# Q, K and V of a hybrid decoder layer: one PSUM bank per half product, the next pair's resident products between streamed ones

## The chip, the cores and the metric

One Trainium2 chip, of which the kernel uses one core. The metric is the device time of one execution in microseconds (us), lower is better. A comparison is made between runs of both kernels on the same chip.

A core has five engines, each with a queue of its own that it works off in order: TensorE (PE in the profile; PEld is its weight loads), VectorE (DVE), ScalarE (ACT), GpSimd (POOL) and SyncE (SP), which here issues all DMAs. [...] Operands lie in SBUF.

## The reference

One layer on 1040 tokens (16 meta tokens and 1024 of `x`), width 1024. The part that the change is about:

```python
xn = rms_norm(h, mix_pre_g[l])
proj = xn @ w_in[l]
...
q = proj[..., OFF_Q:OFF_K].reshape(Bsz, L, SB_HEADS, SB_HEAD_DIM)
k = proj[..., OFF_K:OFF_V].reshape(Bsz, L, SB_HEADS, SB_HEAD_DIM)
v = proj[..., OFF_V:IN_COLS].reshape(Bsz, L, SB_HEADS, SB_HEAD_DIM)
y_ssd = ssd_mixer(z, xbc, dt_raw, conv_w, ...)
y_sb = rms_norm(stick_breaking_attention(q, k, v).reshape(Bsz, L, SB_WIDTH), sb_norm_g[l])
mix = jnp.concatenate([y_ssd, y_sb], axis=-1) @ w_out[l]
```

After it come a residual, and a convolutional feed-forward of 2816 columns with its own norms. `ssd_mixer` is a scan over chunks of 128 tokens; the attention takes, for each query, a product of sigmoids over the keys behind it.

## The kernel before, in words

Float32 products are made of three passes: each operand is split into a high part (`fp32r`) and the rest (`lo`), and high x high, high x low and low x high are summed. ScalarE makes the high part, GpSimd or VectorE the rest.

**Stages.** x is normed and turned (lines 227 to 340) into `xall`, which holds both parts of all 1040 tokens; `xq` is a view of it by block of 128 columns of x, half of the tokens, part and token. Then the projections for the scan of head group 0 (line 877), the scan of group 0 with projections of group 1 as filler (878 to 885), the scan of group 1 with Q, K and V as filler (888 to 891), the attention with the rest of Q, K and V as filler (1156 to 1212), the output projection and the feed-forward.

**Q, K and V** are made two 128-column blocks at a time: 12 pairs (`Blocks`, line 400), in the order (k, q), (v, q), (k, v) for every two head pairs. One pair times x is a 2 x 2 block product (two blocks of output, two halves of the inner dimension; two halves of the tokens), done by Strassen's scheme in Winograd's form with 7 products instead of 8. `QKV` (line 45) gives their order, 1, 2, 6, 5, 3, 7, 4, with the names of their operands. Each is done in two halves `c` of 260 tokens: 14 half products, *steps*, a pair; 168 in all. A step is 12 matmuls of 128 x 128 on 128 x 260 (line 497). What is called M5c0 below is product 5, half 0.

Products 1, 2 and 3 read x itself from `xq` (the operands `b11`, `b21`, `b22`): they are *resident*. Products 6, 5, 7 and 4 read sums of x's quarters (`t2`, `t1`, `t3`, `t4`), which were written to DRAM once (`x_sums`, line 360, to `xt13` and `xt42`) and are *streamed* back: each half product needs one unit of 1040 KB, in two halves. They land in a ring of two units (line 388), which lies where the fourth quarter of x was. `load_half` (392) is called twice in every streamed step, behind the matmuls that read the half to be replaced, and so always loads for the streamed step after next.

PSUM has two banks for this (`psum_mm`, line 75, two buffers), one for each `c`. Products 1 and 2 add up in one bank, 5 and 3, and 7 and 4 too: the flag `first` says which of them starts a sum. Between them the bank is read: after 1 ScalarE copies it to C21 (508), and after 2 the same bank holds C11. VectorE adds the others to what is in SBUF (514 to 525). For a K block, high part and rest are made straight from PSUM (`keep_k`, 470): ScalarE copies, and VectorE subtracts; the list `late` puts these behind the next step's matmuls.

**Weights.** A pair's two raw blocks (512 KB each) are loaded into two buffers (`load`, 405, `wraw`), sums are made of them in place on VectorE (`sums`, 425), and four splits make high part and rest (`split_a`, `split_s12`, `split_s34`, `split_a22`; ScalarE line 413, GpSimd line 414) into three rotating buffers. `qkv_flow` (571) says after which of a pair's 14 steps each of these is put into the program: `split_s34` after step 1 and `split_a22` after step 5 of the pair itself; for the next pair `load(0)` after 3, `load(1)` after 8, `split_a` after 9, `sums` after 10, `split_s12` after 12.

**The order of the work.** In the attention TensorE runs in the order in which the program is written (line 1154). For the other engines and for SP the framework's scheduler chooses an order when the kernel is built: of what it takes to be ready, the earliest in the program. So a load whose buffer it takes to be free can come to stand ahead of loads that are written before it. An engine's queue is then worked off in that order, and an instruction that waits holds up all behind it. `behind` (351) keeps the operations of `x_sums` from going ahead of what was written before on the named engines.

**The attention** takes one block of 128 queries of one head pair at a time (`block_weights`, 920): logits on TensorE (940), two sigmoids on ScalarE (941, 942), a scan on VectorE (948), a product on GpSimd (950, 951); the turning (962) and the product with V (977) come up to three blocks later. Two or three steps of Q, K and V go into each (`run(fill, 1)`). When a head pair is done, the last of it is added up on VectorE (1000) and stored (1001). `turn_v` and `turn_edge` (535, 546) turn V for it.

Of the kernel before, what the change touches and what calls it, by code (L numbers as in the profile page):

```python
# [44 lines left out]
QKV = [(1, "a11", "b11", True), (2, "a12", "b21", False), (6, "s2", "t2", True), (5, "s1", "t1", True),  # L45
       (3, "s4", "b22", False), (7, "s3", "t3", True), (4, "a22", "t4", False)]
# [11 lines left out]
def tile_layer(ctx: ExitStack, tc: tile.TileContext, x, meta, rows, parts,  # L58
# [292 lines left out]
    def behind(*engines):  # L351
        st = ExitStack()
        traced = nc.cur_bb.bb.instructions
        for e in engines:
            last = next((i for i in reversed(traced) if i.engine == e), None)
            if last is not None:
                st.enter_context(tc.issue_after(last))
        return st

    def x_sums(k):  # L360
        rs = []

        def add_up():
            rs.extend(rp.tile([P, 2, HT], F32R, tag="rkl", name=f"xr{j}_{k}", bufs=3).bitcast(F32) for j in range(2))
            r1, r2 = rs
            with behind(ET.Pool):
                for r, kk in ((r1, k), (r2, k + 4)):
                    nc.gpsimd.tensor_tensor(r, xq[:, kk, :, 0].bitcast(F32), xq[:, kk, :, 1].bitcast(F32), op=ALU.add)
                nc.gpsimd.tensor_tensor(r1[:, 0], r1[:, 1], r1[:, 0], op=ALU.subtract)
                nc.gpsimd.tensor_tensor(r1[:, 1], r2[:, 1], r1[:, 1], op=ALU.subtract)  # L370

        def split():
            r1, r2 = rs
            with behind(ET.DVE, ET.Activation):
                nc.vector.tensor_tensor(r2[:, 1], r2[:, 1], r1[:, 0], op=ALU.subtract)
                nc.vector.tensor_tensor(r2[:, 0], r2[:, 0], r2[:, 1], op=ALU.subtract)
                for r, dst, nm in ((r1, xt13, "13"), (r2, xt42, "42")):
                    h = rp.tile([P, 2, HT], F32R, tag="rk", name=f"xh{nm}_{k}", bufs=3)
                    lo = r.bitcast(F32R)
                    nc.scalar.activation(h, r, AF.Copy)  # L380
                    nc.vector.tensor_tensor(lo, r, h.bitcast(F32), op=ALU.subtract)
                    for j, s in enumerate((h, lo)):
                        nc.sync.dma_start(out=dst[:, :, :, k, j, :],
                                          in_=s.bitcast(F32).rearrange("p t (c n) -> p t c n", n=HP))

        return add_up, split

    ring = [xq[:, 0:4, 1].rearrange("p k b n -> p k (b n)")[:, :, 2 * HP * s:2 * HP * s + 2 * HP] for s in range(2)]
# [3 lines left out]
    def load_half():  # L392
        u, h = divmod(loaded[0], 2)
        if u < len(units):
            loaded[0] += 1
            (src, j), c = t_of[units[u][0]], units[u][1]
            ks = slice(2 * h, 2 * h + 2)
            nc.sync.dma_start(out=ring[u % 2][:, ks].bitcast(F32), in_=src[:, j, c, ks].rearrange("p k b n -> p k (b n)"))

    class Blocks:  # L400
        def __init__(self, f1, f2, n):
            self.n, self.src, self.w = n, [{"q": w_q, "k": w_k, "v": w_v}[f][p] for f, p in (f1, f2)], {}
            self.f, self.r, self.late = (f1, f2), [None, None], []
# [21 lines left out]
        def sums(self):  # L425
            r1, r2 = self.r
            self.s2 = rp.tile([P, 4, P], F32, tag="s2", name=f"s2_{self.n}", bufs=1)
            add = nc.vector.tensor_tensor
            add(r1[:, 0:4], r1[:, 0:4], r2[:, 0:4], op=ALU.subtract)
# [34 lines left out]
        def part(self, j, th, c):  # L464
            a = HT * th + HP * c
            if self.f[j][0] == "k":
                return [t[:, a:a + HP] for t in self.d[j]]
            return self.d[j][:, a:a + HP]

        def keep_k(self, th, c, a):  # L470
            kh, kl = self.part(0, th, c)
            acts = [lambda: nc.scalar.activation(kh, a, AF.Copy),
                    lambda: nc.vector.tensor_tensor(kl, a, kh.bitcast(F32), op=ALU.subtract)]
            if th == 0:
                acts.pop(0)()
            self.late += acts

        def step(self, s):
            (n, wn, xn, first), c = QKV[s // 2], s % 2
            if s == 0:  # L480
                self.d = [None, self.dest(1)]
            if s == 2:
                self.d[0] = self.dest(0)
            if first:
                self.acc = getattr(self, "acc", {})
                self.acc[c] = psum_mm(f"pj{n}_{self.n}_{c}")
            acc = self.acc[c]
            hi, lo = self.w[wn]
            if xn[0] == "t":
                rv = ring[used[0] % 2].rearrange("p k (b n) -> p k b n", b=2)  # L490
                used[0] += 1
            else:
                kk, th = {"b11": (0, 0), "b21": (4, 0), "b22": (4, 1)}[xn]
                rv = xq[:, kk:kk + 4, th, :, HP * c:HP * c + HP]
            for k in range(4):
                for j, (w, b) in enumerate(((hi, 0), (hi, 1), (lo, 0))):
                    mm(acc[:, :HP], w[:, k, :], rv[:, k, b, :], start=first and k == 0 and j == 0,  # L497
                       stop=k == 3 and j == 2, skip_group_check=not first)
                if xn[0] == "t" and k % 2:
                    load_half()  # L500
            for act in self.late:
                act()
            self.late = []
            add, a = nc.vector.tensor_tensor, acc[:, :HP]
            c11 = self.part(0, 0, c) if n in (2,) else None
# [3 lines left out]
            elif n == 2 and self.f[0][0] == "k":  # L509
                self.keep_k(0, c, a)  # L510
            elif n == 2:
                nc.scalar.activation(c11, a, AF.Copy)
            elif n == 6:
                add(c21, a, c21, op=ALU.add)
            elif n == 5:
                add(c22, a, c21, op=ALU.add)
            elif n == 3 and self.f[0][0] == "k":
                add(a, a, c21, op=ALU.add)
                self.keep_k(1, c, a)
            elif n == 3:  # L520
                add(self.part(0, 1, c), a, c21, op=ALU.add)
            elif n == 7:
                add(c22, a, c22, op=ALU.add)
            elif n == 4:
                add(c21, a, c21, op=ALU.add)
# [19 lines left out]

    def turn_edge(p):
        q, (kh, kl), v, vc = heads[p]
        vt = vts.pop(p)
        edge = rp.tile([P, NT, NM], F32, tag="edge", name=f"edge{p}", bufs=1)
        nc.vector.tensor_copy(edge[:, :NT - 1, :], vt[:, P:NT * P].rearrange("p (t c) -> p t c", c=P)[:, :, :NM])  # L550
        nc.vector.tensor_copy(edge[:, NT - 1, :], vt[:, T:L])
        tp = psum_tp(f"vtc{p}")
        nc.tensor.transpose(tp[:, 0, :], edge.rearrange("p t c -> p (t c)"), ident)
# [6 lines left out]
    def v_turns(p):  # L560
        return [lambda: turn_v(p, 0), lambda: turn_v(p, 1), lambda: turn_edge(p)]
# [9 lines left out]
    def qkv_flow():  # L571
        post = []
        for n, b in enumerate(blocks):
            nxt = blocks[n + 1] if n + 1 < len(blocks) else None
            (f1, p1), (f2, p2) = b.f
            for s in range(14):
                b.step(s)
                if post and s:
                    post.pop(0)()
                if s == 1:  # L580
                    b.split_s34()
                if s == 5:
                    b.split_a22()
                if nxt:
                    ahead = {3: lambda: nxt.load(0), 8: lambda: nxt.load(1), 9: nxt.split_a, 10: nxt.sums,
                             12: nxt.split_s12}.get(s)
                    if ahead:
                        ahead()
                if s == 9 and f1 == "v":
                    post = v_turns(p1)  # L590
                if nxt is None:
                    left[0] = 2 * ((s > 0) + (s > 2) + (s > 8) + (s > 12))
                    left[1] = int(s > 8)
                yield
            if f2 == "v":
                post = v_turns(p2)
        for act in post[:2] + [lambda: None] * 2 + post[2:]:
            act()
            yield
# [13 lines left out]
    with tc.tile_pool(name="ssd", bufs=1, side="right") as sp:  # L613
# [248 lines left out]
        def scan_steps(g):  # L862
# [3 lines left out]
            for c in range(NT + 1):  # L866
# [7 lines left out]
        parts_ = [x_sums(k) for k in range(4)]  # L874
        posts = [[parts_[0][0]], [parts_[0][1], parts_[1][0]], [parts_[1][1], parts_[2][0]],
                 [parts_[2][1], parts_[3][0], parts_[3][1]]]
# [31 lines left out]
    edges, ys_of = {}, {}  # L908
# [84 lines left out]
    def edge_mix(p, th):  # L993
# [7 lines left out]
        nc.sync.dma_start(out=yd1[:, :, p, :].rearrange("t d c -> d t c"), in_=ysc)  # L1001
# [154 lines left out]
    for p in range(8):  # L1156
        for i in range(NT):
# [11 lines left out]
            run(block)  # L1169
            if (p, i) == (7, 1):  # L1170
# [50 lines left out]
    edge_mix(7, edge)  # L1221
    run(meta_steps)
# [837 lines left out]
```

## Time and profile before

| | us |
|---|---|
| median of 3 runs | 1852.49 |
| lowest, highest | 1851.43, 1856.2 |
| the profiled execution | 1856.6 |
| its span, first to last instruction | 1854.8 |
| start of the first and the last matmul of Q, K and V (line 497) | 335.2, 935.4 |
| granted TensorE clock, mean over the span | 0.968 |

The profile is of one execution. Times in it are counted from the span's start. A row of a group names line, engine, operation, output<-input, shape and count, then its busy time and the mean of one, then the time that the engine stood idle just before it, and who ended that. A row of waits has the total, how often, and the longest. The time of the profiled execution is 4.1 us over the median of the runs.

### The profile page before, as it was taken

The numbers are of one execution on the slowest core, as the hardware profiler recorded it, in microseconds if no ns is written. First come the engines' busy times: TensorE is split into PE (matmuls) and PEld (weight loads), VectorE is DVE, ScalarE is ACT, GpSimd is POOL, SyncE is SP. The second block draws the span as 40 slices with busy tenths as digits, with TensorE's granted clock in tenths as the row PEclk, the third lists the DMA queues.
The fourth block names the chain that finished last, engine by engine and source line by source line (L and its number), as shares of the span: only waits on it lengthen the run. The fifth ranks groups of instructions, "written<-read, shape, count | busy, mean of one in ns | idle before, by whom it ended". The sixth has DMA issues, their size and how long they took to land. (4 is left out here: it accounts for less than half of the span.)

```text
span 1854.8 us, 29414 instructions
## 1 busy us (share of the span) xinstructions
PE 1729.7 (93%) x11518; PEld 1508.0 (81%) x11518; DVE 1233.3 (66%) x1360; ACT 856.6 (46%) x1474; POOL 972.9 (52%) x697
## 2 busy tenths in 40 slices
PE   7999899997888889888899999999999999999998
PEld 6998789876777788777767877898888999888786
DVE  5765884776658758768764056766666666657777
ACT  5424463543555656546665234543333333334544
POOL 4365664575657747667546212458677777600001
PEclk9999899998999989999999999999999999999999
DMA  4235443677665556655722354423223333187335
GB/s 153 69 109 177 146 132 103 206 251 244 216 199 185 196 158 200 218 201 192 239 92 83 133 198 148 137 69 117 95 86 92 118 103 104 61 270 251 103 97 187
DMA packets 151354, 284.73 MB, mean 154 GB/s; under 512 B 14032, under 2 KB 47336, under 8 KB 151216
## 3 DMA queue, kind: packets, MB, share of 16 engines
q1 hardware_dynamic: 151216, 282.85, 46.3%
q8 instruction: 91, 1.49, 0.3%
q14 instruction: 47, 0.39, 0.1%
HBM read 224.56 MB, written 58.25 MB: 152 GB/s over the span
## 5 line engine op out<-in xcount | busy, mean ns | idle before, releaser
L950 POOL TENSOR_TENSOR bt<-bt,kp 128x256 f32<-128x256 f32 (+7 forms) x128 | 210.2, 1660 | 139.9 <-DVE kp L948 110.3
L948 DVE TENSOR_TENSOR_SCAN kp<-kp,hold 128x272 f32<-128x272 f32 (+7 forms) x128 | 209.4, 1676 | 64.6 <-ACT kp L941 47.6
L497 PE MATMUL pj<-xall,whis 128*128 128x260 f32 x768 | 169.9, 319 | 53.0 <-DMA xall<-xt 35.1
L497 PEld LDWEIGHTS pj<-xall,whis 128*128 128x128 f32 x768 | 131.3, 209 | 69.3 <-issue 26.0
L1413 POOL TENSOR_TENSOR wlo<-wr,whi 128x1024 fp32r<-128x1024 f32 x43 | 109.2, 2551 | 37.2 <-ACT whi L1412 37.2
L497 PE MATMUL pj<-xall,whia 128*128 128x260 f32 x576 | 116.3, 300 | 10.2 <-DMA xall<-xt 6.2
L1917 POOL TENSOR_TENSOR fms<-fms 128x1 f32<-128x1 f32 x8 | 2.7, 334 | 223.7 <-DMA ar<-fda 187.5
L497 PE MATMUL pj<-xall,wlos 128*128 128x260 f32 x384 | 116.2, 303 | 0.0
L941 ACT ACTIVATE kp<-z 128x288 f32<-128x288 f32 (+6 forms) x112 | 82.5, 737 | 67.5 <-PE z L940 33.0
L497 PEld LDWEIGHTS pj<-xall,whia 128*128 128x128 f32 x576 | 89.8, 192 | 21.0 <-issue 6.0
L1412 ACT ACTIVATE whi<-wr 128x1024 fp32r<-128x1024 f32 x43 | 45.6, 1060 | 112.5 <-PE fX L1470 68.1
L160 PE MATMUL pj_X<-xall,wh_X 128*128 128x320 f32 (+1 forms) x384 | 96.9, 338 | 0.0
L1542 DVE SCALAR_TENSOR_TENSOR ga<-gr,pp,ga 128x1024 f32<-128x1024 f32 x44 | 71.4, 1622 | 34.0 <-ACT ga L1535 33.1
L964 ACT ACTIVATE th<-tw 128x1024 f32<-128x1024 f32 (+2 forms) x96 | 75.8, 815 | 39.2 <-PE tw L962 37.9
L160 PE MATMUL pj_z<-xall,wh_z 128*128 128x306 f32 (+2 forms) x384 | 92.4, 327 | 0.0
L1802 ACT ACTIVATE dh<-ar 128x512 fp32r<-128x512 f32 x77 | 48.5, 630 | 92.5 <-PE dnB L1880 44.7
L1803 DVE TENSOR_TENSOR dl<-ar,dh 128x512 fp32r<-128x512 f32 x77 | 53.2, 691 | 50.4 <-ACT dh L1802 50.3
L1119 PE MATMUL mo<-xall,yh 128*128 128x512 f32 x256 | 85.7, 402 | 0.0
L962 PE MATMUL tw<-ident,bt 128*128 128x128 f32 x576 | 78.7, 280 | 5.4 <-ACT bt L942 3.1
L942 ACT ACTIVATE bt<-z 128x288 f32<-128x288 f32 (+6 forms) x112 | 82.8, 740 | 0.0
L497 PE MATMUL pj<-xall,wloa 128*128 128x260 f32 x288 | 81.7, 284 | 0.0
L497 PEld LDWEIGHTS pj<-xall,wlos 128*128 128x128 f32 x384 | 80.3, 209 | 0.0
(579 smaller groups left out, 5752.6 us busy)
## 6 DMA issues: line engine op xcount, KB each, us to landing
xall<-xt SPq DMA_DIRECT2D x192, 520.0 KB
wr<-in_w_up SPq DMA_DIRECT2D x44, 512.0 KB
fds<-ga SPq DMA_DIRECT2D x44, 256.0 KB
b<-in_w_down SPq DMA_DIRECT2D x44, 256.0 KB
ar<-fds SPq DMA_DIRECT2D x44, 256.0 KB
fda<-ga SPq DMA_DIRECT2D x33, 256.0 KB
ar<-fda SPq DMA_DIRECT2D x33, 256.0 KB
yk<-yd SPq DMA_DIRECT2D x16, 512.0 KB
```

What stands on the lines that cost most here:

```text
L160: mm(acc[:ncol, :n - s], a[:, k, :ncol], x_cols(k, b, c0 + s, n - s), start=(k == 0 and j == 0), stop=(k == KB - 1 and j == 2))
L497: mm(acc[:, :HP], w[:, k, :], rv[:, k, b, :], start=first and k == 0 and j == 0, stop=k == 3 and j == 2, skip_group_check=not first)
L941: nc.scalar.activation(kp[:, :, a:a + w], z[:, :, :w], AF.Sigmoid, scale=-QSCALE)
L942: nc.scalar.activation(bt[:, :, a:a + w], z[:, :, :w], AF.Sigmoid, scale=QSCALE)
L948: nc.vector.tensor_tensor_scan(kp[:, j][:, ::-1], kp[:, j][:, ::-1], hold[:, L - n:L][:, ::-1], 0.0, op0=ALU.mult, op1=ALU.max)
L950: nc.gpsimd.tensor_tensor(bt[:, j, 0:m], bt[:, j, 0:m], kp[:, j, 1:m + 1], op=ALU.mult)
L962: nc.tensor.transpose(tw[:, j, b, :], bt[:, j, c0:c0 + P], ident)
L964: nc.scalar.activation(th[:, :, :nb, :], tw[:, :, :nb, :], AF.Copy)
L1119: mm(acc, u[:, k, :], v[:, cs], start=(k == 0 and j == 0), stop=(k == 7 and j == 2))
L1413: nc.gpsimd.tensor_tensor(l, raw, h.bitcast(F32), op=ALU.subtract)
L1542: nc.vector.scalar_tensor_tensor(v, self.g[jj][:, :, i:i + 256], fconv_w[:, j, i:i + 1], v, op0=ALU.mult, op1=ALU.add)
L1803: sub(lo[:, k], raw, hi[:, k].bitcast(F32), op=ALU.subtract)
```

## The change

- **Banks.** Each half product starts a sum in a bank of its own, and the bank is free when it has been read once. Products 2 and 3 now get their other term by an add on VectorE; product 7 is added to both C22 and C21. For a K block one add on VectorE empties the bank into a float32 tile `ks` (it shares the one buffer `s2` with the weights' sum S2), and for both halves together ScalarE makes the high part and GpSimd the rest.
- **Order.** From the first pair on, products 1 and 2 of the next pair are done within this one: 6, 5, 3, 7, next 1, 4, next 2. The counting of steps starts at product 6.
- **Weights.** `split_a22` after step 1 (M6c1), `load(0)` after 2, `split_a` after 4, `load(1)` after 5, `sums` after 7, `split_s12` after 9, `split_s34` of the next pair after 12.
- **Half units.** The ring is four pieces; a half unit is 128 runs of 4160 bytes where it was 256 of 2080.
- **x's sums.** All operations of `x_sums` run on VectorE, without `behind`; its tiles alternate between two tags; all of one k is put behind one z block.
- **Smaller.** The columns of V that the last turn needs are copied out right after the second turn (`keep_edge`); the store of a head pair's result (1001) is put behind the rest of the block's logits; when the output projection's weights may overwrite x follows the new order.

```diff
-            with behind(ET.Pool):
-                for r, kk in ((r1, k), (r2, k + 4)):
-                    nc.gpsimd.tensor_tensor(r, xq[:, kk, :, 0].bitcast(F32), xq[:, kk, :, 1].bitcast(F32), op=ALU.add)
...
-                    nc.scalar.activation(h, r, AF.Copy)
+        op2 = nc.vector.tensor_tensor
+        for r, kk in ((r1, k), (r2, k + 4)):
+            op2(r, xq[:, kk, :, 0].bitcast(F32), xq[:, kk, :, 1].bitcast(F32), op=ALU.add)
+        op2(r1[:, 0], r1[:, 1], r1[:, 0], op=ALU.subtract)
+        op2(r1[:, 1], r2[:, 1], r1[:, 1], op=ALU.subtract)
+        op2(r2[:, 1], r2[:, 1], r1[:, 0], op=ALU.subtract)
+        op2(r2[:, 0], r2[:, 0], r2[:, 1], op=ALU.subtract)
+        for r, dst, nm in ((r1, xt13, "13"), (r2, xt42, "42")):
...
+            nc.vector.tensor_copy(h, r)
+            op2(lo, r, h.bitcast(F32), op=ALU.subtract)
...
-    ring = [xq[:, 0:4, 1].rearrange("p k b n -> p k (b n)")[:, :, 2 * HP * s:2 * HP * s + 2 * HP] for s in range(2)]
+    ring = [xq[:, a, 1].rearrange("p b n -> p (b n)") for a in range(4)]
...
-            nc.sync.dma_start(out=ring[u % 2][:, ks].bitcast(F32), in_=src[:, j, c, ks].rearrange("p k b n -> p k (b n)"))
+            nc.sync.dma_start(out=ring[2 * (u % 2) + h].bitcast(F32), in_=src[:, j, c, ks].rearrange("p k b n -> p (k b n)"))
...
+        def keep_k(self, th, c, a, term):
+            if c == 0:
+                self.ks = rp.tile([P, HT], F32, tag="s2", name=f"ks{th}_{self.n}", bufs=1)
+            nc.vector.tensor_tensor(self.ks[:, HP * c:HP * c + HP], a, term, op=ALU.add)
+            if c == 1:
+                kh, kl = (t[:, HT * th:HT * th + HT] for t in self.d[0])
+                nc.scalar.activation(kh, self.ks, AF.Copy)
+                nc.gpsimd.tensor_tensor(kl, self.ks, kh.bitcast(F32), op=ALU.subtract)
...
-            if first:
-                self.acc = getattr(self, "acc", {})
-                self.acc[c] = psum_mm(f"pj{n}_{self.n}_{c}")
-            acc = self.acc[c]
+            acc = psum_mm(f"pj{n}_{self.n}_{c}")
...
+            if n in (2, 3):
+                term = c21 if n == 2 else c22
+                if self.f[0][0] == "k":
+                    self.keep_k(n - 2, c, a, term)
+                else:
+                    nc.vector.tensor_tensor(self.part(0, n - 2, c), a, term, op=ALU.add)
+                return
+            for dst, term in {6: ((c21, c21),), 5: ((c22, c21),), 7: ((c22, c22), (c21, c21)), 4: ((c21, c21),)}[n]:
+                nc.vector.tensor_tensor(dst, a, term, op=ALU.add)
...
+            row = [(b, 6), (b, 5), (b, 3), (b, 7)] + ([(nxt, 1), (b, 4), (nxt, 2)] if nxt else [(b, 4)])
+            acts = {1: [b.split_a22]}
...
+                acts.update({4: [nxt.split_a], 7: [nxt.sums], 9: [nxt.split_s12], 12: [nxt.split_s34]})
...
+                acts[2] = [lambda: nxt.load(0)]
+                acts[5] = [lambda: nxt.load(1)]
...
-        nc.sync.dma_start(out=yd1[:, :, p, :].rearrange("t d c -> d t c"), in_=ysc)
+        stores.append(lambda: nc.sync.dma_start(out=yd1[:, :, p, :].rearrange("t d c -> d t c"), in_=ysc))
...
             run(block)
+            while stores:
+                stores.pop()()
```

More of the change, by code (lines that the diff above doesn't have):

```diff
@@ L499, in step @@
                 if xn[0] == "t" and k % 2:
                     load_half()
[L501 to L505, printed above, removed]
+            a = acc[:, :HP]
             c21, c22 = self.part(1, 0, c), self.part(1, 1, c)
```

166 lines of the change are left out of this document (69 added, 97 removed).

## Prediction

> **What bounds the kernel now.** First the head of the page and its row of busy times:
>
> ```profile
> span 1854.8 us, 29414 instructions
> ...
> PE 1729.7 (93%) x11518; PEld 1508.0 (81%) x11518; DVE 1233.3 (66%) x1360; ACT 856.6 (46%) x1474; POOL 972.9 (52%) x697
> ```
>
> TensorE is busy for 93%, so time is to be won where it stands still. The table by stretches, for the 600 us of Q, K and V, has PE, PEld, DVE, ACT, POOL, granted clock, DMA share:
>
> ```profile
> 335.00:935.00 600.00, 517.54 (x4372) 456.70 (x4371) 431.30 (x505) 332.85 (x635) 393.95 (x299) 0.93 0.64 211
> ```
>
> TensorE stands still for 82.5 us, most of its idle time in the kernel, and the clock is 0.93 where the whole run has 0.968. Who ended those waits say the groups of line 497 (`whis` are the weights of products 6, 5, 3, 7; `whia` those of 1, 2, 4) and the waits:
>
> ```profile
> L497 PE MATMUL pj<-xall,whis 128*128 128x260 f32 x768 | 169.9, 319 | 53.0 <-DMA xall<-xt 35.1 <-DVE kl L473 16.0 <-DVE vt L521 1.0
> L497 PE MATMUL pj<-xall,whia 128*128 128x260 f32 x574 | 115.9, 300 | 10.2 <-DMA xall<-xt 6.2 <-DVE q L525 2.2 <-DVE q L523 1.3
> ```
>
> ```profile
> PE pj L497 <- DVE kl L473: 16.0, 10, 2.9
> ...
> PE pj L497 <- DVE q L525: 2.2, 2, 1.9
> ...
> PE pj L497 <- DVE q L523: 1.3, 1, 1.3
> PE pj L497 <- DVE vt L521: 1.0, 2, 0.8
> PE pj L497 <- DVE q L516: 0.8, 1, 0.8
> ...
> PE pj L497 <- DVE vt L525: 0.5, 1, 0.5
> ```
>
> The ring costs 41.3 us (35.1 under `whis`, 6.2 under `whia`, where only product 4 is streamed), the emptying of banks 21.8. Why the ring is late shows one pair, on the queues of SP, POOL and PE:
>
> ```profile
> 578.96 0.35 SPq L407 DMA_DIRECT2D wr<-in_w_k  x1
> 590.19 0.35 SPq L407 DMA_DIRECT2D wr<-in_w_q  x1
> 590.63 8.04 SPq L398 DMA_DIRECT2D xall<-xt  x6
> ```
>
> ```profile
> 588.73 1.43 POOL L414 TENSOR_TENSOR wloa<-wr,whia 128x512 fp32r<-128x512 f32 x1
> ```
>
> ```profile
> 595.35 0.77 PE L497 MATMUL pj<-xall,whis 128*128 128x260 f32 x2 [5.47 <-DMA xall<-xt]
> ```
>
> `load(1)` of the next pair stands ahead of the loads for M5c0, although it is written four steps behind them. Its buffer comes free when GpSimd ends `split_a22` (590.16); until then SP stands, the ring's loads behind it, and M5c0 waits 5.47 us. So it is the queue's order and GpSimd's lateness, not the bandwidth. Over the stage:
>
> ```profile
> SPq L407 <- POOL wlos L414: 61.9, 10, 12.5
> SPq L407 <- POOL wloa L414: 57.6, 7, 16.1
> ...
> SPq L1001 <- DVE ysc L1000: 17.6, 6, 7.1
> ```
>
> **The change part by part.** The profiled execution took 1856.6 us, 1.8 of it outside its span; the runs' median is 4.1 lower. The sum starts from 1856.6.
>
> *Product 4.* Its units are asked for two steps ahead as before, but with the next pair's product 1 between 7 and 4, two resident steps lie there: four steps. The 6.2 us go: **-6.2** (ends 0 and -6.2). What would be late next, the next pair's M6, also has four steps.
>
> *Products 6 and 5* stay four streamed steps in a row, so M5 still gets its unit two steps after it is asked for. `split_a22` may begin when product 2 ends, and M6 follows product 2 in both kernels: what held up the ring at 590 is still there. Against that, more work for GpSimd lies just ahead of that place (`split_s34` and the rest of K), which the scheduler sees too; where it takes the buffer to come free later, it puts `load(1)` behind the ring's loads, as it did in this earlier pair:
>
> ```profile
> 535.52 1.06 SPq L398 DMA_DIRECT2D xall<-xt  x2
> 536.72 0.38 SPq L407 DMA_DIRECT2D wr<-in_w_v  x1
> 539.78 8.41 SPq L398 DMA_DIRECT2D xall<-xt  x6
> ```
>
> Ends: all 35.1 gone, or each of 11 pairs 1.5 us later (the next paragraph's K rest) and so 16 more. I take 27 left, **-8**. Single pieces carry the same bytes in half the runs; the ring waits for its queue, so nothing is counted. The store of line 1001, moved behind the block, stood ahead of ring loads for part of its 17.6 us; that is within the same ends.
>
> *Banks.* The rest of K was held back by a step and kept its bank: 16.0. Now one add frees it. What other adds cost is 5.8 us (2.2, 1.3, 1.0, 0.8, 0.5) for 104 of them; with 144 banks freed by VectorE I scale to 8.0: **-13.8** (ends: -21.8 and 0, when VectorE is late for all). The adds:
>
> ```profile
> L414 POOL TENSOR_TENSOR wlos<-s,whis 128x512 fp32r<-128x512 f32 x11 | 16.4, 1495 | 6.5 <-ACT whis L413 6.5
> L473 DVE TENSOR_TENSOR kl<-pj,kh 128x260 fp32r<-128x260 f32 x32 | 13.4, 420 | 8.3 <-ACT kh L472 8.3
> L429 DVE TENSOR_TENSOR wr<-wr,wr 128x512 f32<-128x512 f32 x11 | 10.0, 909 | 13.1 <-POOL wloa L414 13.1
> L948 DVE TENSOR_TENSOR_SCAN kp<-kp,hold 128x144 f32<-128x144 f32 (+7 forms) x110 | 181.7, 1692 | 39.6 <-ACT kp L941 35.5 <-issue 2.0 <-POOL bt L950 1.8
> L950 POOL TENSOR_TENSOR bt<-bt,kp 128x128 f32<-128x128 f32 (+7 forms) x110 | 177.7, 1634 | 105.9 <-DVE kp L948 81.2 <-ACT ysc L980 7.0 <-ACT bt L942 5.5
> L917 DVE TENSOR_TENSOR ql<-q,qh 128x128 fp32r<-128x128 f32 x57 | 63.8, 1120 | 1.5 <-ACT qh L916 1.4
> ```
>
> A K pair has 14 adds on VectorE before and after (four subtractions go, two adds for product 2 and two for 7 come; product 3 keeps its two), the four others 10 and 14: 16 x 0.42 = 6.7 us more in 431, beside TensorE. GpSimd gets 16 rests of K, 520 wide: 16 x 1.5 = 24 us more in 394. On the path comes only what waits for it: `sums`, whose tile shares its buffer with `ks`. It stands in VectorE's queue ahead of scans, and GpSimd waits for those. The like wait in the row of line 429 is 13.1; I take **+4** (ends 0 and 13).
>
> *Clock.* Behind a long wait TensorE runs at half clock; the stretch behind the wait at 590:
>
> ```profile
> 594.00:600.00 6.00, 4.65 (x26) 4.20 (x28) 0.43 (x1) 0.64 (x2) 0.00 (x0) 0.50 0.98 353
> ```
>
> 0.07 of 600 us is 42 us of clock withheld for 82.5 idle; part of it falls on the idle time itself, so I take 0.3 us per us of wait: on 28 us removed **-8.5** (ends 0 and -14, all of it). [...]
>
> *What the others take back.* With 36.5 us less of waits and slow clock, VectorE's 431 and GpSimd's 394 have to fit into less time. I let them take back half: **+18** (ends 0 and all).
>
> *x's sums.*
>
> ```profile
> L368 POOL TENSOR_TENSOR xr<-xall x8: 2400/2650/3434, 98.7 to 188.3; 128x1040 f32<-128x1040 f32 x8
> L380 ACT ACTIVATE xh<-xr x8: 1057/1071/1075, 148.3 to 197.7; 128x1040 fp32r<-128x1040 f32 x8
> L381 DVE TENSOR_TENSOR xr<-xr,xh x8: 1226/1236/3379, 149.4 to 199.4; 128x1040 fp32r<-128x1040 f32 x8
> ...
> L369 POOL TENSOR_TENSOR xr<-xr x4: 1652/1966/2292, 104.9 to 179.5; 128x520 f32<-128x520 f32 x4
> L370 POOL TENSOR_TENSOR xr<-xr,xr x4: 1302/1742/2293, 107.3 to 192.1; 128x520 f32<-128x520 f32 x4
> L375 DVE TENSOR_TENSOR xr<-xr,xr x4: 700/2568/2917, 125.1 to 193.5; 128x520 f32<-128x520 f32 x4
> L376 DVE TENSOR_TENSOR xr<-xr x4: 701/1988/2392, 127.4 to 195.2; 128x520 f32<-128x520 f32 x4
> ```
>
> ```profile
> PE sg L784 <- ACT sgh L775: 7.6, 3, 4.3
> ```
>
> ```profile
> 100.00:155.00 55.00, 52.21 (x327) 51.73 (x326) 28.82 (x20) 13.13 (x21) 27.39 (x14) 0.97 0.38 124
> 155.00:215.00 60.00, 47.96 (x260) 42.31 (x260) 47.46 (x37) 29.69 (x61) 44.83 (x24) 0.83 0.55 175
> ```
>
> They last to 199, into the scan's first chunks, where TensorE idles 12 of 60 us at clock 0.83 and waits 7.6 for ScalarE, whose queue holds the copies. On VectorE one k is 2 + 2 + 2 operations of 1040 at 1.24 and 4 of 520 at 0.70, 10.2 us, 41 in all (the plain copy's price is not in the trace: at most that of the subtraction). Without `behind` they may fill the 26 us that VectorE idles before 155. GpSimd is rid of 8 x 2.65 + 4 x 1.97 + 4 x 1.74 = 36, ScalarE of 8.6. **-6** (ends -20, the 12 idle us and the clock, and +6, if the last k stands ahead of the first chunk).
>
> Sum: -6.2 - 8 - 13.8 + 4 - 8.5 + 18 - 6 = -20.5, so 1836.1 against the profiled execution and **1832** against the median.
>
> **The rivals.**
>
> *The ring's loads go first.* `load(1)` comes behind them in all pairs. For: the pair at 536. Against: most later pairs look like 590. Another 27 us and their clock, half taken back: 17 less, 1815.
>
> *Nothing to see.* Waits move to other engines. For: the scans already wait 35.5 us for ScalarE and GpSimd 81.2 for the scans. What is left is x's sums and some of product 4: 1848.
>
> *GpSimd late at the pair's edge: slower.* Between M4 and M6 lie two steps now (product 2 alone) where there were four, and at them `split_s34` (whose end frees the buffer of `load(0)`), the rest of K and `split_a22`. The row below gives 2.3 for the first (two shapes in one mean); with 1.5 for the rest of K the last ends 3.8 us later, both loads stand ahead of the ring on SP, and M5 waits 11 x 3.8 = 42 more. With the 20 of product 4 and the banks gone that is +22, +6.6 of clock, half of it caught up by the other engines: +14, +4 and -6: 1864. It decides once GpSimd ends `split_a22` 2 us later than now in most pairs.
>
> ```profile
> L414 POOL TENSOR_TENSOR wlos<-wr,whis 128x1024 fp32r<-128x1024 f32 (+1 forms) x23 | 53.0, 2305 | 18.1 <-ACT whis L413 18.1
> ```
>
> *Two readers of SBUF.* Scans, rests of Q and GpSimd's work sum to 640 us in 600 (181.7 + 63.8 + 393.95), and line 381 takes 1.24 or 3.38 by what runs beside it. If that rate is a ceiling, 24 us more make the stage 600 x 664/640 = 622, and TensorE's waits only move: +22 - 6, 1868. [...]
>
> **How the numbers follow.** Forecast 0.44 (its own range 1815 to 1846), loads first 0.11, nothing 0.17, GpSimd late 0.18, two readers 0.10. Within 0.3% (5.6 us), about what a measurement can tell here, lies the third alone: faster 0.55, same 0.17, slower 0.28. Range 1808 to 1868: from below the loads-first time, by part of its unknown ends, to both slower rivals' times; what lies beyond them, half of 0.28, and a little below 1808 is left out.
>
> **What would show it.** Right: no DMA wait in a row of product 4, none for the rest of K, under 10 us for adds; line 497's waits for the ring near 27, at M5; clock above 0.94; waits of `sums` for GpSimd; no `sg` wait by 215. Wrong: SP's waits at line 407 above 120 us with ring waits above 41; or VectorE's scans and GpSimd's products longer per piece while TensorE waits for adds.

## The result and the profile after

| | before | after |
|---|---|---|
| median of 3 runs, us | 1852.49 | 1830.15 |
| lowest, highest | 1851.43, 1856.2 | 1829.2, 1831.84 |
| the profiled execution | 1856.6 | 1829.2 |
| ratio after / before | | 0.9876, 95% interval 0.9852 to 0.9900 |

The change is faster by 22.3 us. The page of the changed kernel begins with:

```profile
span 1827.5 us, 29461 instructions
PE 1723.5 (94%) x11518; PEld 1504.8 (82%) x11518; DVE 1228.7 (67%) x1400; ACT 845.3 (46%) x1442; POOL 951.5 (52%) x697
```

The span is 27.3 us shorter than before's, and TensorE's busy time only 6.2 us. To see where the time went, the run is cut at two places: the first matmul of Q, K and V, and the first of the output projection (`mo`), behind which only the tail of the layer is left. Both are in the rows of a source line (count, shortest/median/longest in ns, start of the first and of the last). Before:

```profile
L497 PE MATMUL pj<-xall,whia x576: 277/283/1207, 335.2 to 935.3; 128*128 128x260 f32 x192
L1119 PE MATMUL mo<-xall,yh x256: 388/393/505, 954.5 to 1085.7; 128*128 128x512 f32 x128
```

After (lines 497 and 1119 are now 478 and 1111):

```profile
L478 PE MATMUL pj<-xall,whia x576: 277/283/683, 312.6 to 904.2; 128*128 128x260 f32 x192
L1111 PE MATMUL mo<-xall,yh x256: 387/393/505, 927.1 to 1058.1; 128*128 128x512 f32 x128
```

Q, K and V begin 22.6 us earlier. From there to the output projection it was 619.3 us and is 614.5: **4.8 us are won where most of the change was made, and 22.6 ahead of it**, where only x's sums were changed. The table by stretches says how. After, columns as in the prediction:

```profile
100.00:155.00 55.00, 53.45 (x344) 52.92 (x343) 43.41 (x46) 11.70 (x19) 14.84 (x9) 1.00 0.79 255
155.00:215.00 60.00, 60.00 (x386) 53.53 (x385) 46.36 (x45) 35.87 (x76) 40.13 (x26) 1.00 0.37 111
312.60:927.10 614.50, 537.66 (x4528) 472.45 (x4526) 437.83 (x535) 342.85 (x634) 419.90 (x325) 0.93 0.61 208
```

The last of these stretches before:

```profile
335.20:954.50 619.30, 534.52 (x4528) 468.62 (x4526) 448.12 (x519) 345.92 (x658) 406.55 (x309) 0.93 0.62 207
```

In the 60 us from 155 TensorE stood 12.04 us and ran at 0.83; now it is never idle, at 1.00. That is 12.0 us of idle time and up to 10 of clock (0.17 x 60), nearly all of the 22.6. VectorE does more work from 100 to 155 (43.41 for 28.82). x's sums in the rows of three of their lines:

```profile
L357 DVE TENSOR_TENSOR xr<-xall x8: 1221/1232/1243, 31.8 to 130.9; 128x1040 f32<-128x1040 f32 x8
L365 DVE CAST xh<-xr x8: 687/690/2081, 110.4 to 139.8; 128x1040 fp32r<-128x1040 f32 x8
L366 DVE TENSOR_TENSOR xr<-xr,xh x8: 1225/1230/1244, 112.2 to 140.5; 128x1040 fp32r<-128x1040 f32 x8
```

They run from 32 to 142 us, where they ran from 99 to 201, and are done before TensorE begins the scan of group 0 (its first matmul is at 155.4).

In the Q, K and V part TensorE's idle time went from 84.8 (619.3 - 534.52) to 76.8 (614.5 - 537.66), and the clock stayed at 0.93. Who ended TensorE's waits after the change, from the groups of line 478 and the waits in 312 to 904:

```profile
L478 PE MATMUL pj<-xall,whis 128*128 128x260 f32 x768 | 166.0, 314 | 36.7 <-DMA xall<-xt 21.6 <-DVE ks L454 7.9 <-DVE vt L491 2.8
L478 PE MATMUL pj<-xall,whia 128*128 128x260 f32 x574 | 116.2, 300 | 9.7 <-DVE q L494 6.9 <-DVE vt L494 2.4
```

```profile
PE pj L478 <- DVE q L494: 9.3, 8, 2.8
PE z L932 <- ACT th L956: 8.9, 3, 3.8
...
PE vtp L512 <- DVE vt L494: 4.2, 2, 2.8
```

TensorE now waits 21.6 us for the ring, where it waited 41.3, and none of it under `whia`, product 4. The rest of K is in neither row. But the adds (9.3, 7.9, 2.8 and 2.4) cost 22.4, where they and the rest of K cost 21.8 before; and the waits of V's turn (4.2) and of the sigmoids' chain (8.9, 2.0 before) have grown. SP's waits ahead of the weights' loads (line 389) and VectorE's for the rest of K on GpSimd:

```profile
SPq L389 <- POOL wlos L396: 46.3, 8, 9.1
SPq L389 <- POOL wloa L396: 40.6, 9, 9.0
```

```profile
DVE meta_k L528 <- POOL kl L458: 18.1, 6, 4.1
DVE wr L412 <- POOL wloa L396: 12.6, 5, 3.6
DVE s L414 <- POOL kl L458: 11.0, 5, 4.1
```

At these loads SP stands 86.9 us where it stood 119.5. VectorE has a wait that the prediction didn't name: `meta_k`, 16 columns of K, stands in its queue behind a rest of K that is now made on GpSimd.

### The profile page after: what moved, and what is told of

Its sections match the earlier page's. It is cut to its first block, busy times and chain, and to the rows that moved or that the text cites. A ratio compares the mean times of both kernels' runs of the same rounds, so it can differ in the third digit from the quotient of the medians.

```text
span 1827.5 us, 29461 instructions
## 1 busy us (share of the span) xinstructions
PE 1723.5 (94%) x11518; PEld 1504.8 (82%) x11518; DVE 1228.7 (67%) x1400; ACT 845.3 (46%) x1442; POOL 951.5 (52%) x697
## 5 line engine op out<-in xcount | busy, mean ns | idle before, releaser
L940 DVE TENSOR_TENSOR_SCAN kp<-kp,hold 128x272 f32<-128x272 f32 (+7 forms) x128 | 205.2, 1644 | 59.4 <-ACT kp L933 45.0
L478 PE MATMUL pj<-xall,whis 128*128 128x260 f32 x768 | 166.0, 314 | 36.7 <-DMA xall<-xt 21.6
L160 PE MATMUL pj_X<-xall,wh_X 128*128 128x320 f32 (+1 forms) x384 | 92.8, 327 | 0.0
L969 PE MATMUL av<-th,v 128*64 128x128 f32 x1152 | 85.2, 298 | 0.0
```

The lines of the kernel that those rows point to most:

```text
L160: mm(acc[:ncol, :n - s], a[:, k, :ncol], x_cols(k, b, c0 + s, n - s), start=(k == 0 and j == 0), stop=(k == KB - 1 and j == 2))
L478: mm(acc[:, :HP], w[:, k, :], rv[k][:, b, :], start=k == 0 and j == 0, stop=k == 3 and j == 2)
L940: nc.vector.tensor_tensor_scan(kp[:, j][:, ::-1], kp[:, j][:, ::-1], hold[:, L - n:L][:, ::-1], 0.0, op0=ALU.mult, op1=ALU.max)
L969: mm(av[halves[j], :], v[:, kb, halves[j]], th[:, j, b, :], start=kb == 0, stop=kb == i)
```

## The experiments

Two questions were open. First, what x's sums alone are worth, and why so much. Theory A reads the traces as above (22 us for x's sums, 5 for Q, K and V); theory B keeps the prediction's sizes (6 and 14). Second, what holds Q, K and V back now: SP's queue (called theory A too), or the other engines, to which TensorE's waits only move (theory C). Each ratio is to before in the same set of runs, with its 95% interval.

### x's sums alone

The kernel before, with `x_sums` and its places (`posts`) from the change, nothing else.

> The kernel before with x's sums alone taken from the change (all on VectorE, without `behind`, two tags, one k behind one z block). Theory A (read from the two traces: the first matmul of Q, K and V comes 22.6 us earlier, and from there to the first matmul of the output projection only 4.8 us are gained): 22 us faster than before, about 1830, and Q, K and V as in before (600 us from the first to the last matmul of their line). Theory B (the prediction's sizes: 6 for x's sums, 14 for the banks and the order): about 1846, and Q, K and V begin some 6 us earlier.

Measured: **0.9896 (0.9876 to 0.9916)**, 1834.04 against 1855.68. Its stretch from the first matmul of Q, K and V (313.7) to the output projection (935.2):

```profile
313.70:935.20 621.50, 533.25 (x4526) 465.85 (x4525) 448.73 (x519) 346.10 (x658) 407.64 (x309) 0.93 0.62 206
```

It takes 621.5 us (619.3 before) and begins 21.5 us earlier. Theory A holds: x's sums give 19.3 us (15.6 to 23.0) of the 23.0 that the ratio 0.9876 would be here.

### x's sums as before

The changed kernel with `behind`, `x_sums` and `posts` of before.

> The changed kernel with x's sums as before (GpSimd, ScalarE, VectorE, `behind`). Theory A: 1847 to 1850, with the first matmul of Q, K and V at about 335 again; banks, order and single pieces are worth 3 to 5 us together. Theory B: 1838, banks and order worth 14.

Measured: **0.9972 (0.9956 to 0.9988)**, 5.2 us faster than before (2.2 to 8.2), outside theory B's 14. Q, K and V begin at 335.8 again. Its stretch of the scan's first chunks looks like before's again:

```profile
155.00:215.00 60.00, 48.78 (x261) 43.24 (x261) 47.46 (x36) 29.89 (x61) 44.93 (x24) 0.84 0.54 177
```

Four of the traces now have the same Q, K and V part: the changed kernel's, this one and the two that follow. From its first matmul to the output projection they took 614.5, 611.2, 613.3 and 609.6 us; with the old part it was 619.3 (before) and 621.5 (x's sums alone). So a single trace tells this stretch only to about 5 us, and the 4.8 above stands for something between 5 and 12.

### The engine, or the early start

Two kernels take one half of that edit back each. The first has the change's places and no `behind`, but before's engines:

```diff
-            op2(r, xq[:, kk, :, 0].bitcast(F32), xq[:, kk, :, 1].bitcast(F32), op=ALU.add)
-        op2(r1[:, 0], r1[:, 1], r1[:, 0], op=ALU.subtract)
-        op2(r1[:, 1], r2[:, 1], r1[:, 1], op=ALU.subtract)
+            nc.gpsimd.tensor_tensor(r, xq[:, kk, :, 0].bitcast(F32), xq[:, kk, :, 1].bitcast(F32), op=ALU.add)
+        nc.gpsimd.tensor_tensor(r1[:, 0], r1[:, 1], r1[:, 0], op=ALU.subtract)
+        nc.gpsimd.tensor_tensor(r1[:, 1], r2[:, 1], r1[:, 1], op=ALU.subtract)
...
-            nc.vector.tensor_copy(h, r)
+            nc.scalar.activation(h, r, AF.Copy)
```

> The changed kernel with the four additions and subtractions of x's sums back on GpSimd and the plain copies back on ScalarE, still without `behind`, in the places and tags of the change. If the gain comes from the time at which the sums may start (theory A1: in the changed kernel they run from 34 to 142 us, in before from 99 to 199), little is lost: 1830 to 1834. If it comes from the work taken off GpSimd and ScalarE (theory A2: 36 us of GpSimd and 8.6 of ScalarE ahead of the scan, whose first chunks wait for both), 1838 to 1850.

Measured: **0.9942 (0.9923 to 0.9961)**, about 12 us slower than the changed kernel. Its stretch from 100 to 155 us, then a wait of TensorE up to 155 that is 1.9 in the changed kernel, and VectorE's waits at x's sums from 30 to 160:

```profile
100.00:155.00 55.00, 45.76 (x265) 45.17 (x264) 34.87 (x28) 17.46 (x23) 24.94 (x13) 0.88 0.55 180
```

```profile
PE tt_X L635 <- DVE xtk L631: 9.2, 2, 5.5
```

```profile
DVE xr L360 <- POOL xr L359: 11.5, 3, 4.9
...
DVE xr L360 <- POOL craw_X L207: 7.3, 1, 7.3
```

TensorE stands for VectorE (`xtk`), and VectorE stands at an operation of x's sums for GpSimd, 18.8 us. The second kernel stays on VectorE and takes `behind` back:

```diff
     def x_sums(k):
+        with behind(ET.DVE):
+            x_sums_(k)
+
+    def x_sums_(k):
```

> The changed kernel with `behind` put back for x's sums on VectorE, so that they can't go ahead of what is written before them on that engine. Theory A1 (the early start): most of the gain is lost, 1842 to 1850. Theory A2 (the engine): 1830 to 1834.

Measured: **0.9887 (0.9868 to 0.9906)**, within the intervals the changed kernel's. Its sums start late:

```profile
L370 DVE TENSOR_TENSOR xr<-xall x8: 1221/1232/3448, 121.0 to 157.2; 128x1040 f32<-128x1040 f32 x8
```

So on one engine the early start is worth nothing that can be measured; on three engines the early start, with the new places and tags, may be worth some 5 us (0.9972 to 0.9942, whose intervals overlap a little). Theory A2 holds: the engines are the larger part. The reason is argued from the traces and not shown by a run: the sums were a chain over three engines, and in before's 98 to 215 us VectorE stood 27.4 us for the other two, with work of the scan and the projections queued behind:

```profile
DVE xr L381 <- ACT xh L380: 15.1, 1, 15.1
DVE xr L375 <- POOL xr L370: 12.3, 3, 6.8
```

No run parts this standing from the work itself that GpSimd and ScalarE are rid of.

### The load behind the ring's loads

The changed kernel, with the second block's load kept on SP behind the ring's loads written before it (at both places of `acts[5]`, `behind` as in before):

```diff
+    def load_behind(b):
+        with behind(ET.SP):
+            b.load(1)
...
-                acts[5] = [lambda: nxt.load(1)]
+                acts[5] = [lambda: load_behind(nxt)]
```

> The changed kernel with the second block's load for the next pair (`load(1)`) queued on SP behind the ring's loads that are written before it, so that its wait for GpSimd holds up none of them. The changed kernel's ratio to before is 0.9876, and its waits for the ring are 21.6 us. Theory A (the ring's waits come from the order of SP's queue and cost what they show): under 10 us of ring waits are left and the ratio is 0.980 to 0.983 (1815 to 1820 where before is 1852.5). Theory C (in Q, K and V the other engines set the pace, and TensorE's waits only move to another releaser): the ring waits fall too, others rise by as much, ratio 0.986 to 0.989.

Measured: **0.9781 (0.9763 to 0.9800)**, 1814.39 us against 1854.49, even a little under theory A's range. From its first matmul of Q, K and V to the output projection, the ring's waits over the run (line 487), SP's for the block loads (line 398), and TensorE's for others:

```profile
313.40:909.30 595.90, 522.28 (x4526) 458.76 (x4525) 446.93 (x535) 341.70 (x634) 422.58 (x325) 0.95 0.63 215
```

```profile
L487 PE MATMUL pj<-xall,whis 128*128 128x260 f32 x768 | 156.2, 301 | 26.1 <-DMA xall<-xt 9.3 <-DVE ks L463 7.9 <-DVE vt L503 3.8
```

```profile
SPq L398 <- POOL wlos L405: 44.5, 8, 9.1
```

```profile
PE pj L487 <- DVE q L503: 13.7, 7, 5.6
PE z L945 <- ACT th L969: 10.0, 4, 3.7
...
PE pj L487 <- DVE vt L503: 7.3, 3, 3.8
```

SP no longer waits for `wloa`; the ring costs 9.3 us, from 21.6. The stretch is 18.6 us shorter than the changed kernel's. Yet TensorE's idle time fell only from 76.8 to 73.6: the adds of Q and V (13.7 and 7.3, from 9.3 and 2.4) and the sigmoids' chain (10.0 from 8.9) rose by 10.4, as theory C said. The rest goes with the clock, 0.95 for 0.93. Both theories had a part; the price of a wait is told in the last section.

### The order of the products undone

The changed kernel with `qkv_flow` going 1, 2, 6, 5, 3, 7, 4 and the weights' work at before's places; each half product keeps its own bank:

```diff
+            for s in range(14):
+                b.step((1, 2, 6, 5, 3, 7, 4)[s // 2], s % 2)
```

> The changed kernel with the order of the products and the places of the weights' work as in before (1, 2, 6, 5, 3, 7, 4); each half product keeps a bank of its own, single pieces, x's sums on VectorE, late stores. It tells what the banks alone do. By the prediction's sizes banks are worth 13.8 of wait and the order 14.2 (6.2 under product 4 and 8 under 6 and 5); by theory A each is worth about half of the 4 to 8 us that the Q, K and V part gained, ratio 0.988 to 0.990, with waits for the ring near 41 again and those for the rest of K gone. If the order does nothing, the ratio is that of the changed kernel, 0.9876. If the banks do nothing or harm, 0.990 or more.

Measured: **0.9864 (0.9841 to 0.9886)**: no difference to the changed kernel. The rows of its line:

```profile
L478 PE MATMUL pj<-xall,whis 128*128 128x260 f32 x768 | 163.2, 310 | 37.9 <-DMA xall<-xt 20.3 <-DVE q L494 5.2 <-DVE ks L454 4.6
L478 PE MATMUL pj<-xall,whia 128*128 128x260 f32 x576 | 119.1, 304 | 19.4 <-DVE q L494 9.5 <-DMA xall<-xt 6.2 <-DVE vt L494 3.5
```

Product 4 waits 6.2 us for the ring again, as in before: that term of the prediction was a true wait, and it is not seen in the time. Products 6 and 5 wait 20.3 without the new order, where the prediction had let the order bring 35.1 to 27. The new order does shorten SP's waits at the block loads (66.3 + 52.3 here, 86.9 with it), but that doesn't reach TensorE.

### Two pieces

The ring and `load_half` of before (256 runs of 2080 bytes) in the changed kernel.

> The changed kernel with the ring as in before: two units, a half unit in 256 runs of 2080 bytes. The prediction counted nothing for the single pieces: ratio 0.9866 to 0.9886, waits for the ring within 5 us of 21.6. Rival: the time of the runs matters (158 ns for one of 4160 bytes against twice 85 for two of 2080, 7% more work for the DMA engines), the ring comes later in the stretches where the DMA engines are busiest, ring waits of 30 or more, ratio 0.990 or more.

Measured: **0.9848 (0.9831 to 0.9866)**, waits for the ring 22.1 under `whis`. (The medians in the traces are 161 ns for a run of 4160 bytes and 85 for one of 2080.) The single pieces are worth nothing that can be measured (the intervals overlap); the rival, 0.990 or more, is out.

### No loads for the ring after the first two units

The changed kernel; the products read what lies in the ring, so its output is not the layer's.

```diff
-            nc.sync.dma_start(out=ring[2 * (u % 2) + h].bitcast(F32), in_=src[:, j, c, ks].rearrange("p k b n -> p (k b n)"))
+            if u < 2:
+                nc.sync.dma_start(out=ring[2 * (u % 2) + h].bitcast(F32), in_=src[:, j, c, ks].rearrange("p k b n -> p (k b n)"))
```

> The changed kernel without the ring's loads after the first two units: products 6, 5, 7 and 4 read what lies there, so Q, K and V are not the reference's; all else is as in the changed kernel. It shows what the ring can cost at most. Theory A: no wait for the ring, SP's other loads come early, clock and waits recover: 25 to 35 us less than the changed kernel, ratio 0.968 to 0.974. Theory C: waits on VectorE, ScalarE and GpSimd rise instead, 10 us or less, ratio above 0.982.

Measured: **0.9752 (0.9732 to 0.9773)**, 1808.51 us, between the two theories and nearer to theory A. Its stretch and the first of TensorE's waits:

```profile
312.70:906.20 593.50, 520.54 (x4528) 458.26 (x4526) 434.75 (x535) 341.68 (x634) 424.17 (x325) 0.95 0.15 47
```

```profile
PE z L933 <- ACT th L957: 12.8, 8, 5.7
PE pj L479 <- DVE q L495: 11.9, 7, 3.1
PE pj L479 <- DVE ks L455: 9.8, 5, 4.5
```

Without these loads TensorE still stands 73.0 us (593.5 - 520.54). That is what the other engines set, and `load_behind` already comes within 2.4 us of this stretch. By the whole runs it is 5.4 us (0.9781 to 0.9752, whose intervals overlap). So the queue's order was most of what the ring cost, and bandwidth little: the mean share of the DMA engines falls from 0.63 there to 0.15, and this is all that it gives.

### VectorE's new waits

Two kernels take away VectorE's waits for the rest of K. One adds `meta_k` on GpSimd:

```diff
-        nc.vector.tensor_tensor(meta_k[:, p, :], kh[:, 0:NM].bitcast(F32), kl[:, 0:NM].bitcast(F32), op=ALU.add)
+        nc.gpsimd.tensor_tensor(meta_k[:, p, :], kh[:, 0:NM].bitcast(F32), kl[:, 0:NM].bitcast(F32), op=ALU.add)
```

> The changed kernel with one small operation moved: `meta_k` (16 columns of K, 0.17 us a head pair) is added on GpSimd and not on VectorE. In the changed kernel VectorE stands 18.1 us in 6 places for the rest of K that GpSimd now makes, right ahead of this operation, and 11.0 us ahead of the third operation of `sums`; in before neither wait was there. If VectorE's standing costs TensorE (the adds that free the banks come 21.8 us late by the trace, more than the 8 of the prediction), 3 to 8 us less than the changed kernel, ratio 0.983 to 0.986. If VectorE would wait for TensorE or the sigmoids there anyway, ratio 0.986 to 0.989 as the changed kernel has it.

The other makes the rest of K on VectorE:

```diff
-                nc.gpsimd.tensor_tensor(kl, self.ks, kh.bitcast(F32), op=ALU.subtract)
+                nc.vector.tensor_tensor(kl, self.ks, kh.bitcast(F32), op=ALU.subtract)
```

> The changed kernel with the rest of K made on VectorE (16 operations of 520 columns, some 0.7 us each) and not on GpSimd (1.34 us each, 21.5 in all). The prediction let GpSimd's added work cost 4 us at `sums` and part of the 18 that the other engines take back. If that was right, ratio 0.980 to 0.985 (no wait of `sums` or `meta_k` for GpSimd, splits of weights earlier). If GpSimd has room for it and VectorE none, 0.988 to 0.992.

Measured: **0.9848 (0.9827 to 0.9868)** and **0.9858 (0.9829 to 0.9887)**. The first lies just below the changed kernel's interval and inside the range that was given for a cost of VectorE's standing, the second between its two ranges; both intervals overlap the changed kernel's, so neither gain (5 and 3 us) is clear of noise. In the first VectorE's 18.1 us are gone, and the adds still cost TensorE the same:

```profile
PE pj L478 <- DVE q L494: 9.7, 8, 2.8
PE pj L478 <- DVE ks L454: 8.0, 6, 4.3
```

So the standing at `meta_k` isn't what makes the adds late, and the choice of engine for the rest of K matters little, if at all. What in VectorE's queue does make them late stays open. `load_behind` and `meta_k` on GpSimd together:

> `load(1)` behind the ring's loads (ratio 0.9781 before) and `meta_k` on GpSimd together. If the waits of VectorE count, 0.974 to 0.977; if not, 0.977 to 0.980. It is the candidate for the fastest of these kernels.

Measured: **0.9775 (0.9749 to 0.9802)**, no more than `load_behind` alone.

### Two edits of the kernel before

x's sums on VectorE as in the first experiment, and `load_behind`, in the kernel before; banks, order, pieces and stores as they were. Of the second edit:

```diff
-                    ahead = {3: lambda: nxt.load(0), 8: lambda: nxt.load(1), 9: nxt.split_a, 10: nxt.sums,
+                    ahead = {3: lambda: nxt.load(0), 8: lambda: load_behind(nxt), 9: nxt.split_a, 10: nxt.sums,
```

> The kernel before with x's sums on VectorE and `load(1)` behind the ring's loads, with before's shared banks, order and two-piece units. It tells what banks and order are worth once SP's queue holds up nothing. If the queue was all that Q, K and V lost, 0.978 to 0.981, as with the new banks and order; if the banks (18 us of waits for the rest of K, which stay here) count for what they show, 0.985 or more; a ratio of 0.989 would say that without the new order this load does not matter.

Measured: **0.9767 (0.9754 to 0.9781)**, 1812.72 us: as fast as the best with everything else changed, and faster than the changed kernel by about 1%. Beside x's sums alone (0.9896), the one line for the load is worth some 24 us here; banks and order, worth about 5 us without that line, are worth nothing with it. Its stretch and rows:

```profile
313.70:909.30 595.60, 521.95 (x4527) 456.36 (x4525) 453.59 (x519) 345.44 (x658) 405.90 (x309) 0.96 0.65 215
```

```profile
L488 PE MATMUL pj<-xall,whis 128*128 128x260 f32 x768 | 159.4, 305 | 33.3 <-DVE kl L464 17.9 <-DMA xall<-xt 7.9 <-DVE q L505 3.6
L488 PE MATMUL pj<-xall,whia 128*128 128x260 f32 x576 | 118.3, 303 | 16.6 <-DVE q L514 6.2 <-DMA xall<-xt 5.0 <-DVE vt L514 3.4
```

The rest of K still costs 17.9 here, and it costs nothing in the time: TensorE stands 73.65 us, `load_behind` with the new banks 73.62.

## Why the prediction came out right, and where it was wrong

The time, 1832 for 1830.15, is right by luck: two errors cancel. By place: Q, K and V were to give 14.5 (-6.2 - 8 - 13.8 + 4 - 8.5 + 18) and gave 4.8 in the two traces, 5.2 (2.2 to 8.2) by the runs; x's sums were to give 6 and gave 22.6 in the traces, 19.3 by the runs.

- **Product 4, -6.2.** As forecast: no wait for the ring stands in its row, and with the old order the 6.2 are back.
- **Products 6 and 5, 35.1 to 27.** 21.6 were left. The cause as put, SP's queue order behind GpSimd's split, is shown: with the load behind the ring's, 9.3 are left. That the new order, or the rest of K on GpSimd, would help it was wrong: under `whis` 20.3 are left with the old order, 20.3 with the rest of K on VectorE and 20.0 with x's sums as before, but 30.3 with the old banks and only x's sums changed. So it came with the new banks or one of the smaller changes that all those kernels share (the later store is one); no run parts these.
- **Banks, -13.8: this term failed.** The rest of K went, and the adds rose from 5.8 to 22.4, where 8.0 was scaled from the count of adds. The price doesn't scale with the count. More work isn't the reason either: VectorE's busy time in the stretch fell from 448.12 to 437.83, where the prediction had it rise by 6.7. What stands ahead of an add in VectorE's queue is left as the likely reason, and no run shows what it is. The end that the text gave, 0, was the right value.
- **`sums` for GpSimd, +4.** VectorE's waits in `sums` rose from 13.1 to 23.6 (12.6 and 11.0), with 18.1 more at `meta_k`, which the forecast didn't name. No experiment finds a clear price for them in the time.
- **Clock, -8.5: failed.** It is 0.93 as before. A fixed price of 0.3 us per us of wait has the wrong form (last section).
- **What the others take back, +18.** The right kind of term: idle time stays at 73 us even with no ring at all. Its size can't be told from that of the banks: the waits of the matmul's line fell by 16.8 (63.2 to 46.4), the idle time by 8.0.
- **x's sums, -6: this term was mis-sized.** Its end of -20 named the place and the amount, 12 us of idle time and the clock; the working counted engines' work (36 us off GpSimd), not the 27.4 us in which VectorE stood at these operations for two other engines. That the chain cost more than the work is a reading of the rows; no run parts the two.

Of the rivals, "nothing to see" had the mechanism of Q, K and V, waits that move to other engines with about 5 us left; its 1848 is wrong because it left only 4.5 us for x's sums and product 4 together. "The ring's loads go first" was priced at 1815 and didn't happen with this change; when it was made to happen, it gave 1814.39, though not by its sum: the ring's waits fell by 12.3 and not 27, and most of the gain goes with the clock. "GpSimd late at the pair's edge" didn't come: SP's waits at the block loads fell by 32.6. Of "two readers of SBUF" nothing is seen: GpSimd's busy time rose by 13 in the stretch, scans and products kept their lengths (1655 for 1692 ns, 1665 for 1634), and the stretch got shorter. The rate that it took for a possible ceiling is none: scans, rests of Q and GpSimd's work came to 640 us in 600 before, and with `load_behind` to 649 in 575 (181.4 + 56.6 + 411.19). For single instructions the traces show different lengths by what runs beside them: one of line 381's eight took 3379 ns in before (median 1236), and it ran from 167.00 us, beside GpSimd's line 147 from 165.94 to 169.29. Two more, from 149.37 and 164.84 us, took 2260 and 2239 ns, beside GpSimd's work for 1.16 and 2.24 us of it, and the five that had GpSimd's work beside them for 0.13 us at most took 1226 to 1243. In the changed kernel line 366's eight took 1225 to 1244 ns, with GpSimd busy for 14.84 of 55 us; one of them had its line 147 beside it for 1.19 us and took 1237, so it is not so each time. That the reading of SBUF is what they share was the rival's assumption; no run shows it. Of the signs, the ones for product 4, the rest of K, `sums` and `sg` came; "under 10 us for adds" and "clock above 0.94" didn't.

## What to carry to other kernels

A short chain of operations spread over three engines can hold up each queue while it stands for the others (here VectorE's, for 27.4 us): look for the engines' waits at such lines before counting their load, and put the chain on one engine if that one has room. A load whose buffer comes free late belongs behind the loads that must not wait, by an order that is written down; here that one line, worth some 24 us in the kernel before, did more than new banks and a new order, and made them superfluous. What a wait of the busiest engine costs is not its length in the profile, since other waits can take its place (with `load_behind` the ring's waits fell by 12.3 us and the idle time by 3.2): run the kernel without the resource once, and see how much idle time is left.

## What the runs showed of the hardware

In these traces the clock's price of a wait isn't proportional to it: the changed kernel has less idle time in Q, K and V (76.8 us for 84.8), and no less time at half clock (92.2 for 88.7). In the clock record of the traces of before and after, half speed begins only at points of a fixed grid of 3.413 us and lasts 3.41, 6.83 or 10.24 us, but for the last stretch, which ends with the record. Four neighbouring cells of that grid in the changed kernel, with one wait of 2.37 us for an add in the second:

```profile
579.77:583.19 3.42, 3.20 (x26) 2.99 (x26) 3.13 (x4) 1.39 (x5) 1.62 (x3) 1.00 0.45 122
583.19:586.60 3.41, 1.26 (x10) 1.26 (x11) 2.85 (x7) 0.85 (x2) 3.41 (x5) 1.00 1.01 366
586.60:590.01 3.41, 3.41 (x24) 2.84 (x25) 0.76 (x2) 1.58 (x4) 0.71 (x2) 0.50 0.35 141
590.01:593.43 3.42, 3.42 (x29) 3.01 (x27) 2.81 (x4) 3.19 (x7) 1.05 (x1) 1.00 0.41 121
```

TensorE is idle for 2.15 of the second cell's 3.41 us, and the third runs at half clock although TensorE is busy in all of it. Counted over Q, K and V of before and after, each cell at full clock with more than 2.02 us idle (25 cells) was followed by one at half clock, and with one exception none with less than 1.6; a cell at half clock with more than 0.5 us idle was followed by another. Single waits of 1.83 and of 2.37 us in the changed kernel were followed by half speed, though between 1.6 and 2.02 us of idle time in a cell it went both ways.

This fits both odd results. The changed kernel has 8.0 us less idle time than before, but both have 18 stretches at half clock (88.7 us before, 92.2 after). With `load_behind` the idle time fell by only 3.2 more, but there are 14 stretches, 58.0 us (granted clock 0.95 in its 595.9 us); half of the 34.2 us that they are shorter is 17.1, and with the 3.2 that is 20.3 for the 18.6 won; some of the half-clock time is itself idle and counted twice. Of the changed kernel's nine stretches of 6.83 us four go with waits for the ring of 2.6 to 4.4 us; of the three that are left with `load_behind`, none does (its longest wait for the ring is 1.8 us). Single runs of one kernel differ too: the five of `meta_k` on GpSimd with `load_behind` go from 1807.83 us (granted clock 0.984) to 1822.6 (0.976), each slower one at a lower clock. Whether that comes from where their waits fall in the grid, no run shows.
